# Forty dense blocks of a hybrid decoder step computed in pairs by seven half-size products

## The chip, the core and the metric

The kernel runs on one core of a Trainium2 chip. The metric is the device time of one execution in microseconds; the median of several runs is compared. One execution was also profiled: its records give the span from the first to the last instruction, the busy time of each engine and what each one waited for. The engines are named as in the profile: PE (TensorE, the matrix engine; PEld are its weight loads), DVE (VectorE), ACT (ScalarE), POOL (GpSimd) and SP (SyncE, which here issues all DMA transfers). Matmuls write to PSUM; PSUM is read by DVE and ACT, not by POOL.

## The reference, cut to what matters

One inference step of a decoder with two layers for 512 prompt tokens and 8 x 8 sample tokens, 576 in all, at width 2048. Layer A is gated linear attention, layer B a sliding-window attention.

```python
# layer A
proj = rmsnorm(h, g_norm) @ w_in                   # q, k, v, r (output gate), low-rank gate
o = rmsnorm(gla_chunked(q, k, v, logg, s0), g_onorm) * silu(r)
h = h + o @ w_out                                  # first output projection, 2048 x 2048
# layer B
k, v = split(rmsnorm(h, g_norm_kv) @ w_kv)
q, z = split(rmsnorm(h, g_norm_b) @ w_in)          # z: the last gates, 2048 x 2048
o = sink_attention(q, k, v) * silu(z)
h = h + o @ w_out                                  # last output projection, 2048 x 2048
y = rmsnorm(h, g_final)
```

All tensors are float32.

## The kernel before

The activations stand transposed in SBUF: 16 tiles `X[k]` of 128 features (the contraction) by 576 tokens, each as a high and a low part, since the product of two float32 matrices is made of three products of a shorter format: high x high, high x low, low x high. `HP` holds 16 tiles of the same shape in full float32, four to a tile. `halves` splits the 576 tokens into two sides of 288 (`HT`).

**Dense blocks.** `dense` (L184) makes one block, 128 outputs by 576 tokens. It loads the weights in two halves of 512 KB (`load_w`, L171), splits them by quarters of 128 x 512 (`split_w`, L167: a cast on ACT, then a subtraction on DVE), and issues 16 x 3 x 2 matmuls of 288 columns. The two sides of the tokens go to two PSUM banks, in turns. The quarters have `WB` = 4 buffers, so that ACT and DVE can be four quarters ahead of PE. At the end `evac` takes the block out of PSUM.

```python
def dense_mm(p, k, wh, wl, sides):
    x = X[k]
    for w, part in ((wh, 0), (wh, 1), (wl, 0)):
        for a in sides:
            mm(p[:, a, :HT], w, x[:, part, a * HT:(a + 1) * HT], ...)
```

**Stages.** 113 dense blocks follow one another, each of the following at a stretch: the projections of layer A (32 blocks), its output gates (`r_phase`, L665, 16 blocks), the first output projection (`out_a`, L691, 16 blocks with weights wOA), the shared K and V (4), the queries of layer B (`q_phase`, L975, 16), its gates (`z_phase`, L979, 16), and the last output projection (weights wOB, L1000 onward: 13 plain blocks, then 3 by halves of the tokens, 320 and 256 columns, so that norm and store of the first half run under the products of the second). Between stages `split_plain` or `split_gain` (L96 to L102) turn `HP` into the operands `X` of the next stage, one ACT and one DVE operation of 576 columns for each of 16 tiles.

**Side chains.** The recurrent part of layer A and the attention of layer B (`attention`, L952: 64 units of two heads and one block of queries, and 16 units for the samples, four in flight on the four PSUM banks of `bank`) are generators. `run` (L199) traces a dense stage and advances the side chains by a given number of steps for each step of it (0.95 for the attention); `drain` (L208) traces what is left of them. Tile orders the instructions of each engine when the program is built (`schedule_with_timeline_sim`, L1165): an instruction traced later can be put ahead of one that is not ready.

**Evictions.** A gate block is evicted in four steps: L984 (x 0.5 and the norm, from PSUM), a Tanh on ACT (L986), L987 and L988 on DVE (in layer A: L670 to L674). A block of the first output projection adds the residual (L700), which came by DMA, goes to DRAM as `dh1`, and its square is added to the sum for the next norm: L114 on ACT, L119 on POOL.

Of the kernel before, what the change touches and what calls it, by code (L numbers as in the profile page):

```python
# [17 lines left out]
D = 2048  # L18
NP = 512
NT = 576  # L20
# [17 lines left out]
def kernel(ctx: ExitStack, tc: tile.TileContext, A, O):  # L38
# [102 lines left out]
    def rstd_soon(srcs, n, b, lo, hi):  # L141
        """the same for the sum of srcs, left in the first bank of b; by columns, for few tokens"""
        toks = range(lo, hi, 128)
        col = sp.tile([128, 4], F32, tag="col", name=nm("col"))
# [9 lines left out]
        for i in range(m):  # L154
            dg = sp.tile([128, 128], F32, tag="dg", name=nm("dg"), bufs=2)
            vec.tensor_scalar(dg, ident, col[:, i:i + 1], None, ALU.mult)
            mm(p[:, i * 128:(i + 1) * 128], ones, dg, start=True, stop=True)
# [38 lines left out]

    bgs = []

    def run(fg):  # L199
        """trace fg, with the steps of the background chains between its own"""  # L200
# [17 lines left out]
    dqkb = [tc.dram_tile([6, 128, NT], F32, name=f"dqkb{h}") for h in range(NH)]  # L218
    dv = [tc.dram_tile([4, 128, NT], F32, name=f"dv{h}") for h in range(NH)]
    dh1 = tc.dram_tile([KT, 128, NT], F32, name="dh1")  # L220

    xT = A["xT"]
    rstdA = cp.tile([128, NT], F32, name="rstd", tag="rstd")

    with tc.tile_pool(name="gp", bufs=1) as gp:
        # ================= layer A ========================================
# [15 lines left out]
        rA2 = halves(rstdA)  # L242
# [21 lines left out]
        # low-rank gate: the columns [wh | wl] three times, so that the rows of its  # L264
        # output carry what the stacked operand of the next product needs
# [9 lines left out]
        # the first two blocks and the gate's product, together as x comes in  # L275
# [902 lines left out]
```

## Time and profile before

| what | value |
|---|---|
| median of 3 runs | 1792.68 us (1792.38 to 1793.38) |
| span of the profiled execution | 1791.2 us |
| PE busy, matmuls | 1767.2 us (99%), 13152 |
| DVE busy, instructions | 1117.0 us (62%), 2539 |
| ACT busy | 780.5 us (44%) |
| POOL busy | 110.1 us (6%) |
| granted PE clock, mean | 0.996 |
| HBM | 174.57 MB read, 43.65 MB written |

The span runs from the first to the last instruction; what a run's time has beyond it lies around the span. The times of three runs lie within 1.0 us. A busy share is a mean over all stages; the groups of rows below take single stages. A matmul's recorded duration holds the whole passage through the engine, and matmuls overlap, so that the distance between two starts is less than the duration.

### The profile page before, as it was taken

To read this page: it belongs to the slowest core of one execution; us is meant where nothing else is said; L and a number is where in the kernel's file an instruction comes from. 1 tells how busy PE (TensorE), PEld (TensorE's weight loads), DVE (VectorE), ACT (ScalarE), POOL (GpSimd) and SP (SyncE) were. 2 spreads that over 40 slices of the span, in tenths; PEclk is the share of its full clock that TensorE was granted. 3 is DMA by queue.
4 is the path that set the end of the run, shared out by engine and by line. 5 is a ranking of instruction groups with operands and counts; after the bars stand their busy time and mean duration, and the time that the engine had idled before them with its cause. 6 is when DMAs were issued, how large, how long until landed. Compare 5 with 4: busy or idle time off the path is not lost.

```text
span 1791.2 us, 33731 instructions
## 1 busy us (share of the span) xinstructions
PE 1767.2 (99%) x13152; PEld 1748.8 (98%) x13152; DVE 1117.0 (62%) x2539; ACT 780.5 (44%) x1632; POOL 110.1 (6%) x190
## 2 busy tenths in 40 slices
PE   8999999999999999999999999999999999999997
PEld 7999999999999999999999999999999999999996
DVE  8576776786776886544222566888888873442234
ACT  7533334334444344343222555667666652332231
POOL 3000001001001001000010100100000000001110
PEclk9999999999999999999999999999999999999998
DMA  8245643564564343223333444343332222223323
GB/s 301 89 160 176 195 156 117 176 197 136 161 194 158 119 154 135 96 77 124 128 131 127 134 134 110 88 126 101 105 99 88 85 94 82 83 98 108 104 106 106
DMA packets 118767, 231.02 MB, mean 129 GB/s; under 512 B 22064, under 2 KB 49584, under 8 KB 118576
## 3 DMA queue, kind: packets, MB, share of 16 engines
q1 hardware_dynamic: 118608, 228.88, 39.4%
q8 instruction: 103, 1.69, 0.4%
q14 instruction: 56, 0.46, 0.1%
HBM read 174.57 MB, written 43.65 MB: 122 GB/s over the span
## 4 chain that ended last, share of the span: by engine, by line
PE 94%; issue 2%; DMA 2%; DVE 1%; ACT 0%; POOL 0%; POOLq 0%; DVEq 0%; SPq 0%; ACTq 0%
PE pd L180 79%; PE pb L463 2%; PE pb L863 1%; PE pb L550 1%; DMA hp<-in_xT_dram 1%; PE pb L846 1%; PE pb L639 1%; PE pb L638 1%; PE pb L636 1%; PE pb L845 1%; PE pb L551 1%; PE pb L873 1%; PE pb L874 1%; PE pb L481 1%; PE pb L558 0%
## 5 line engine op out<-in xcount | busy, mean ns | idle before, releaser
L180 PE MATMUL pd<-x,wh 128*128 128x288 f32 x7232 | 1305.0, 298 | 9.8 <-ACT x L96 6.7
L180 PEld LDWEIGHTS pd<-x,wh 128*128 128x128 f32 x7232 | 1080.2, 189 | 17.4 <-ACT x L96 6.7
L180 PE MATMUL pd<-x,wl 128*128 128x288 f32 x3616 | 791.8, 298 | 0.7 <-DVE wl L169 0.6
L180 PEld LDWEIGHTS pd<-x,wl 128*128 128x128 f32 x3616 | 587.6, 189 | 4.1 <-DVE wl L169 1.4
L168 ACT CAST wh<-raw 128x512 fp32r<-128x512 f32 x452 | 279.4, 618 | 589.8 <-PE pd L180 577.5
L169 DVE TENSOR_TENSOR wl<-raw,wh 128x512 fp32r<-128x512 f32 x452 | 316.4, 701 | 337.7 <-ACT wh L168 336.1
L119 POOL TENSOR_TENSOR acc<-acc,st 128x576 f32<-128x576 f32 x46 | 70.3, 1528 | 323.2 <-ACT st L114 322.4
L855 ACT ACTIVATE s<-s,tiny 128x257 f32<-128x257 f32 (+1 forms) x128 | 60.9, 478 | 19.8 <-DVE tiny L853 19.6
L618 ACT CAST sh<-Si 128x512 fp32r<-128x512 f32 x64 | 39.7, 620 | 66.9 <-PE pb L638 43.9
L114 ACT ACTIVATE st<-hp 128x576 f32<-128x576 f32 (+2 forms) x66 | 43.3, 664 | 56.8 <-DVE hp L1045 28.6
L117 POOL COPY acc<-st 128x576 f32<-128x576 f32 x7 | 5.5, 779 | 907.6 <-ACT st L114 907.6
L640 DVE SCALAR_TENSOR_TENSOR Si<-Si,dl,pb 128x512 f32<-128x512 f32 x64 | 47.6, 744 | 12.2 <-PE pb L636 11.4
L619 DVE TENSOR_TENSOR sl<-Si,sh 128x512 fp32r<-128x512 f32 x64 | 44.4, 693 | 13.6 <-PE pb L639 5.5
L850 DVE SCALAR_TENSOR_TENSOR s<-distp,pb 128x256 f32<-128x256 f32 (+1 forms) x128 | 43.9, 383 | 11.2 <-PE pb L846 10.6
L867 ACT CAST pTh<-pb 128x256 fp32r<-128x256 f32 (+1 forms) x64 | 34.0, 532 | 29.7 <-PE pb L863 28.2
L868 DVE TENSOR_TENSOR pTl<-pb,pTh 128x256 fp32r<-128x256 f32 (+1 forms) x64 | 39.6, 620 | 8.4 <-ACT pTh L867 7.7
L878 ACT COPY hp<-pb 64x128 f32<-64x128 f32 x128 | 33.3, 260 | 25.5 <-PE pb L874 14.7
L438 ACT ACTIVATE E<-E 128x2304 f32<-128x2304 f32 (+1 forms) x20 | 37.5, 1875 | 15.3 <-DVE E L435 15.3
L97 DVE SCALAR_TENSOR_TENSOR x<-hp,c_vecs,x 128x576 fp32r<-128x576 f32 x48 | 42.1, 913 | 2.0 <-ACT x L96 2.0
L879 DVE TENSOR_TENSOR hp<-hp,pb 64x128 f32<-64x128 f32 x128 | 36.2, 283 | 9.2 <-ACT hp L878 6.6
L863 PE MATMUL pb<-c_ident,s 128*128 128x128 f32 x224 | 40.6, 273 | 0.0
L853 DVE TENSOR_REDUCE tiny<-s 128x2 f32<-128x258 f32 (+1 forms) x64 | 39.3, 616 | 1.7
(234 smaller groups left out, 1803.2 us busy)
## 6 DMA issues: line engine op xcount, KB each, us to landing
raw<-in_wA_dram SPq DMA_DIRECT2D x92, 512.0 KB
raw<-in_wB_dram SPq DMA_DIRECT2D x64, 512.0 KB
Si<-in_state_dram SPq DMA_DIRECT2D x64, 256.0 KB
out_gla_sample_dram<-Si SPq DMA_DIRECT2D x64, 256.0 KB
raw<-in_wOA_dram SPq DMA_DIRECT2D x32, 512.0 KB
raw<-in_wOB_dram SPq DMA_DIRECT2D x32, 512.0 KB
dqkb<-st SPq DMA_DIRECT2D x24, 288.0 KB
hp<-in_xT_dram SPq DMA_DIRECT2D x16, 288.0 KB
```

What stands on the lines that cost most here:

```text
L97: vec.scalar_tensor_tensor(t[:, 1, :], src, g, f32(t[:, 0, :]), ALU.mult, ALU.subtract)
L114: act(sq[:, lo:hi], src, AF.Square)
L119: self.eng.tensor_tensor(self.acc[:, lo:hi], self.acc[:, lo:hi], sq[:, lo:hi], ALU.add)
L168: nc.scalar.copy(wh, raw)
L169: vec.tensor_tensor(wl, raw, f32(wh), ALU.subtract)
L180: mm(p[:, a, :HT], w, x[:, part, a * HT:(a + 1) * HT], start=(k == 0 and w is wh and part == 0), stop=(k == KT - 1 and w is wl))
L618: nc.scalar.copy(sh, Si)
L619: vec.tensor_tensor(sl, Si, f32(sh), ALU.subtract)
L640: vec.scalar_tensor_tensor(Si, Si, dl[:, f * 16 + i:f * 16 + i + 1], p, ALU.mult, ALU.add)
L850: vec.scalar_tensor_tensor(s[:, e, off:256], distp[:, off:256], slope(2 * m + e), p[:, e * 256 + off:(e + 1) * 256], ALU.mult, ALU.subtract)
L855: act(s[:, e, off:257], s[:, e, off:257], AF.Exp, scale=-1.0, bias=tiny[:, e:e + 1], accum_out=tiny[:, 2 + e:3 + e])
L863: nc.tensor.transpose(out=p[:, (hf * 2 + e) * 128:(hf * 2 + e + 1) * 128], in_=s[:, e, off + hf * 128:off + (hf + 1) * 128], identity=ident)
```

## The change

Two neighbouring blocks (256 outputs), the 2048 features in two halves and the 576 tokens in two halves make a product of 2 x 2 by 2 x 2 parts. Before, it takes eight half-size products; now it takes seven, by Strassen's scheme in Winograd's form. Sums of weight halves (s1 to s4, eight additions of 128 x 512 per pair, on POOL, in place of the loaded weights) and sums of operand parts (t1 to t4, made once for each stage) come in addition, and the results are put together from the seven. Pairs are: all 16 blocks of wOA, gate blocks 4 to 15 of layer B, blocks 0 to 11 of wOB. Around them: the last six gate blocks of layer A move behind the release of that layer's memory, and the operand sums for wOA stand among them; the attention is drained after two gate blocks of layer B, two more plain ones follow with the operand sums of h read back from `dh1` (`sums_of_h`, `t1_of_h`), then come six gate pairs; before wOB `make_t` makes the operand sums of the gated attention; t1 takes the place of one operand part in `X`, so that the first half of the gated attention's second token half goes to DRAM (`dg2`) and is loaded again for the last four blocks, of which two (not three) go by halves. Sums of squares in the paired stages are added on DVE. The rest of the diff (removed comments, moved definitions) is left out.

```diff
+    PRODUCTS = {"A": ("w11", "x11", 0), "P4": ("w22", "t4", 1), "B": ("w12", "x21", 0),
+                "P5": ("s1", "t1", 2), "P6": ("s2", "t2", 3), "C": ("s4", "x22", 2),
+                "P7": ("s3", "t3", 1)}
+    ORDER = [(n, c) for n in ("A", "P4", "B", "P5", "P6", "C", "P7") for c in range(2)]
+    FIRST = [("A", 0), ("P4", 0), ("P5", 0), ("P6", 0), ("A", 1), ("P4", 1), ("B", 0), ("B", 1),
+             ("P5", 1), ("P6", 1), ("C", 0), ("C", 1), ("P7", 0), ("P7", 1)]
+    def dense_pair(wdram, blk, pool, evac, order=ORDER):
+        for name, b, hf in (("w11", 0, 0), ("w22", 1, 1), ("w12", 0, 1), ("w21", 1, 0)):
...
+        place = {"s1": "w22", "s2": "w11", "s3": "w21", "s4": "w12"}
...
+        def add(out, a, b, c):
+            nc.gpsimd.tensor_tensor(half(out, c), half(a, c), half(b, c), ALU.add)
+        def ready(c):
+            if ("w22", c) in split and ("s1", c) not in made:
+                add("s1", "w21", "w22", c)
+            if ("w11", c) in split and ("s1", c) in made and ("s2", c) not in made:
+                add("s3", "w11", "w21", c)
+                add("s2", "s1", "w11", c)
+            if ("w12", c) in split and ("s2", c) in split and ("s4", c) not in made:
+                add("s4", "s2", "w12", c)
+        for n, c in order:
...
+            split_w(half(w, c), wh, wl)
+            ready(c)
+            for kk in range(4):
+                for wt, part in ((wh, 0), (wh, 1), (wl, 0)):
+                    mm(p, wt[:, kk, :], xpart(x, k, part), ...)
...
+            if ends[n] == 2:
+                evac(n, p)
+    def make_t(g, lo, hi, tmp):
+        x11, x12, x21, x22 = lo[:, :, 0:HT], lo[:, :, HT:NT], hi[:, :, 0:HT], hi[:, :, HT:NT]
...
+        nc.gpsimd.tensor_tensor(t3, x22, x12, ALU.subtract)
+        vec.tensor_tensor(x12, x11, x12, ALU.subtract)
+        vec.tensor_tensor(t2, x12, x22, ALU.add)
+        nc.gpsimd.tensor_tensor(t4, t2, x21, ALU.subtract)
+        split("t4", t4)
+        split("t2", t2)
+        split("t3", t3)
+    def pair_out(j, r, ss, store):
+        def f(n, p):
...
+            elif n == "B":
+                vec.tensor_tensor(h[0][:, 0:HT], p, r[0][:, 0:HT], ALU.add)
...
+            elif n == "C":
+                vec.tensor_tensor(h[0][:, HT:NT], p, r[0][:, HT:NT], ALU.subtract)
+                ss.add(h[0])
+            elif n == "P7":
+                vec.tensor_tensor(h[1][:, 0:HT], r[1][:, 0:HT], p, ALU.subtract)
+                vec.tensor_tensor(h[1][:, HT:NT], h[1][:, 0:HT], tmp["a"][:, 1, :], ALU.add)
+                ss.add(h[1])
...
-        run(r_phase())
+        run(r_phase(range(RS)))
         drain()
+        for g, (a, b) in enumerate(((RS, RS), (RS, 12), (12, 14), (14, KT))):
+            run(r_phase(range(a, b)))
+            for _ in make_t(g, *two(g), tt):
+                pass
         for k in range(KT):
             split_plain(k, hpt(k))
-        ss = SumSq(nc.gpsimd)
+        ss = SumSq(vec)
+        run(out_pairs(A["wOA"], range(0, KT, 2), lambda j: xT[j * 128:(j + 1) * 128, :], ss, True))
...
+    def sums_of_h():
+        for g in range(4):
+            for k in (2 * g, 2 * g + 1):
...
+                    dma(x[i], dh1[kk])
+                    act(x[i], x[i], AF.Copy, scale=vecs[:, GB + kk:GB + kk + 1])
...
         bgs.append([attention(), 0.95, 0.0])
         run(q_phase())
-        run(z_phase())
+        run(z_phase(range(2)))
         drain()
-    NB = 3
+    NB, NS = 2, 12
+    with tc.tile_pool(name="zp", bufs=1) as zp:
+        bgs.append([sums_of_h(), 1.5, 0.0])
+        run(z_phase(range(2, 4)))
+        drain()
+        t1_of_h()
+        for j in range(4, KT, 2):
+            run(dense_pair(A["wB"], KT + j, zp, pair_z(j)))
+        for g in range(4):
+            for _ in make_t(g, *two(g), tt):
+                pass
         for k in range(KT):
             split_plain(k, hpt(k))
+        run(out_pairs(A["wOB"], range(0, NS, 2), lambda j: dh1[j], ss, False))
...
-        for j in range(KT - NB):
+        for j in range(NS, KT - NB):
             run(dense(A["wOB"], j, ev_o(j, resid(j))))
```

`RS` is 10. `pair_z` evicts a gate pair in the same way, with the norm, the Tanh and the product of L984 to L988 at the end.

## Rows read from the trace of the kernel before

**Rows 1.** The page, part 1: busy time, share of the span, instructions.
```profile
PE 1767.2 (99%) x13152; PEld 1748.8 (98%) x13152; DVE 1117.0 (62%) x2539; ACT 780.5 (44%) x1632; POOL 110.1 (6%) x190
```
**Rows 2.** The page, part 5, costliest groups: count, busy us, mean ns, idle before.
```profile
L180 PE MATMUL pd<-x,wh 128*128 128x288 f32 x7232 | 1305.0, 298 | 9.8 <-ACT x L96 6.7
...
L168 ACT CAST wh<-raw 128x512 fp32r<-128x512 f32 x452 | 279.4, 618 | 589.8 <-PE pd L180 577.5
```
**Rows 3.** Timeline of DVE in the first output projection: start us, us, instruction.
```profile
846.39 0.76 DVE L700 TENSOR_TENSOR hp<-pd,ld 128x576 f32<-128x576 f32 x1 [2.07 <-PE pd L180]
...
872.00 0.76 DVE L700 TENSOR_TENSOR hp<-pd,ld 128x576 f32<-128x576 f32 x1 [2.07 <-PE pd L180]
```
**Rows 4.** Timeline of PE, last blocks by halves, equal matmuls merged.
```profile
1739.70 4.56 PE L1041 MATMUL pd<-x,w 128*128 128x320 f32 x30
...
1763.20 13.30 PE L1041 MATMUL pd<-x,w 128*128 128x256 f32 x109
```
**Rows 5.** Timelines of POOL and DVE; then L169 as a line: ns min/median/max.
```profile
711.66 1.43 POOL L119 TENSOR_TENSOR acc<-acc,st 128x576 f32<-128x576 f32 x1 [1.49 <-ACT st L114]
...
712.05 1.58 DVE L169 TENSOR_TENSOR wl<-raw,wh 128x512 fp32r<-128x512 f32 x1 [0.41 <-ACT wh L168]
...
564.07 5.65 POOL L119 TENSOR_TENSOR acc<-acc,st 128x576 f32<-128x576 f32 x3
...
566.31 0.75 DVE L562 SCALAR_TENSOR_TENSOR S<-S,dl,pb 128x512 f32<-128x512 f32 x1
...
L169 DVE TENSOR_TENSOR wl<-raw,wh x452: 669/691/1923, 5.7 to 1727.7; 128x512 fp32r<-128x512 f32 x151
```
**Rows 6.** Line L453 (256 columns), and four queued operations of 576 columns.
```profile
L453 DVE TENSOR_TENSOR E<-E,kb x52: 414/419/423, 124.2 to 663.5; 128x256 f32<-128x256 f32 x52
...
800.72 2.76 DVE L102 TENSOR_TENSOR x<-hp,x 128x576 fp32r<-128x576 f32 x4
```
**Rows 7.** Windows: length, busy PE, PEld, DVE, ACT, POOL, clock, DMA share, GB/s.
```profile
100.00:270.00 170.00, 170.00 (x1235) 166.64 (x1235) 123.00 (x320) 61.30 (x108) 0.00 (x0) 1.00 0.54 174
820.00:1012.00 192.00, 192.00 (x1442) 192.00 (x1441) 59.40 (x85) 56.17 (x89) 20.56 (x15) 1.00 0.37 127
1402.00:1470.00 68.00, 68.00 (x534) 68.00 (x533) 55.34 (x147) 41.91 (x122) 3.27 (x15) 1.00 0.18 63
1720.00:1791.00 71.00, 58.26 (x436) 57.62 (x434) 31.33 (x67) 14.29 (x24) 3.58 (x3) 0.93 0.30 104
```
**Rows 8.** Groups by line in 1402 to 1470 us, dense work alone.
```profile
L180 PE MATMUL pd<-x,wh 128*128 128x288 f32 x263 | 48.8, 299 | 0.0
...
L180 PE MATMUL pd<-x,wl 128*128 128x288 f32 x131 | 29.6, 299 | 0.0
...
L169 DVE TENSOR_TENSOR wl<-raw,wh 128x512 fp32r<-128x512 f32 x17 | 11.6, 684 | 2.0 <-ACT wh L168 1.6 <-PE pb L863 0.3
...
L984 DVE SCALAR_TENSOR_TENSOR st<-pd,rstdB 128x576 f32<-128x576 f32 x5 | 3.8, 751 | 0.1
...
L987 DVE SCALAR_TENSOR_TENSOR st<-st,st 128x576 f32<-128x576 f32 x4 | 3.0, 753 | 0.0
L988 DVE TENSOR_TENSOR hp<-hp,st 128x576 f32<-128x576 f32 x4 | 3.0, 753 | 0.0
```
**Rows 9.** Last results of the attention (first and last start); gate evictions in 1338 to 1404.
```profile
L948 DVE TENSOR_TENSOR hp<-hp,t x32: 195/222/249, 1169.2 to 1468.7; 64x64 f32<-64x64 f32 x32
...
L984 DVE SCALAR_TENSOR_TENSOR st<-pd,rstdB 128x576 f32<-128x576 f32 x4 | 3.0, 748 | 0.3 <-PE pd L180 0.3
```
**Rows 10.** Timeline of DVE at the end: evictions of the last blocks by halves.
```profile
1758.96 0.49 DVE L1045 TENSOR_TENSOR hp<-pd,r 128x320 f32<-128x320 f32 x1 [5.46 <-PE pd L1041]
...
1775.66 0.42 DVE L1045 TENSOR_TENSOR hp<-pd,r 128x256 f32<-128x256 f32 x1
1776.53 0.42 DVE L1045 TENSOR_TENSOR hp<-pd,r 128x256 f32<-128x256 f32 x1 [0.46 <-PE pd L1041]
```

More of the change, by code (lines that the diff above doesn't have):

```diff
@@ L197, with out_pairs @@
+    def out_pairs(wdram, js, src, ss, store):
+        for j in js:
+            r = [tpool[0].tile([128, NT], F32, tag="ld", name=nm("ld"), bufs=2) for _ in range(2)]
+            for i in range(2):
+                dma(r[i], src(j + i))
+            yield from dense_pair(wdram, j, tpool[0], pair_out(j, r, ss, store), FIRST if j == 0 else ORDER)
     bgs = []
@@ L220, with r_phase, ev, f @@
     dh1 = tc.dram_tile([KT, 128, NT], F32, name="dh1")
+    dg2 = tc.dram_tile([8, 128, HT], F32, name="dg2")
+    dt1 = tc.dram_tile([8, 128, HT], F32, name="dt1")
     xT = A["xT"]
     rstdA = cp.tile([128, NT], F32, name="rstd", tag="rstd")
+    rA2 = halves(rstdA)
+    norm_done = [False] * NH
+    def r_phase(js):
+        def ev(j):
+            def f(p):
+                assert norm_done[j // 4]
+                rs = st()
+                vec.scalar_tensor_tensor(halves(rs), p, 0.5, rA2, ALU.mult, ALU.mult)
+                th = st()
+                act(th, rs, AF.Tanh)
+                vec.scalar_tensor_tensor(rs, th, 1.0, rs, ALU.add, ALU.mult)
+                vec.scalar_tensor_tensor(hpt(j), hpt(j), vecs[:, GO + j:GO + j + 1], rs, ALU.mult, ALU.mult)
+            return f
+        for j in js:
+            yield from dense(A["wA"], 32 + j, ev(j))
+    RS = 10
     with tc.tile_pool(name="gp", bufs=1) as gp:
@@ L241 @@
         bmask = const("bmask", [128, 4])
-        rA2 = halves(rstdA)
         def evac_to(dst, scale):
@@ L663, in gla_samples @@
                 norm_done[h] = True
-        def r_phase():
-            def ev(j):
-                def f(p):
-                    assert norm_done[j // 4]
-                    rs = st()
-                    vec.scalar_tensor_tensor(halves(rs), p, 0.5, rA2, ALU.mult, ALU.mult)
-                    th = st()
-                    act(th, rs, AF.Tanh)
-                    vec.scalar_tensor_tensor(rs, th, 1.0, rs, ALU.add, ALU.mult)
-                    vec.scalar_tensor_tensor(hpt(j), hpt(j), vecs[:, GO + j:GO + j + 1], rs, ALU.mult, ALU.mult)
-                return f
-            for j in range(KT):
-                yield from dense(A["wA"], 32 + j, ev(j))
         bgs.append([gates(), 0.5, 0.0])
@@ L718, with gate, z_phase, ev @@
     dk = tc.dram_tile([4, 2, 64, NT], F32, name="dk")
+    units_done = [0]
+    def gate(j, rs):
+        th = st()
+        act(th, rs, AF.Tanh)
+        vec.scalar_tensor_tensor(rs, th, 1.0, rs, ALU.add, ALU.mult)
+        vec.tensor_tensor(hpt(j), hpt(j), rs, ALU.mult)
+        if j < 8:
+            dma(dg2[j], hpt(j)[:, HT:NT])
+    def z_phase(js):
+        def ev(j):
+            def f(p):
+                assert units_done[0] >= min(20 * (j // 4) + 23, 82)
+                rs = st()
+                vec.scalar_tensor_tensor(halves(rs), p, 0.5, rB2, ALU.mult, ALU.mult)
+                gate(j, rs)
+            return f
+        for j in js:
+            yield from dense(A["wB"], KT + j, ev(j))
@@ L720, with t1_of_h @@
+    def t1_of_h():
+        for g in range(4):
+            t = tt()
+            dma(t, dt1[2 * g:2 * g + 2].rearrange("a p t -> p a t"))
+            for i in range(2):
+                o = X[2 * g + i]
+                nc.scalar.copy(o[:, 0, HT:NT], t[:, i, :])
+                vec.tensor_tensor(o[:, 1, HT:NT], t[:, i, :], f32(o[:, 0, HT:NT]), ALU.subtract)
     with tc.tile_pool(name="ap", bufs=1) as ap:
@@ L1054 @@
             else:
-                r = rstd_soon([ss.acc, sq], D, (1, 2, 3), lo, hi)
+                r = rstd_soon([ss.acc, sq], D, (1, 2, 3), lo, hi, tp)
             for j in range(KT):
```

185 lines of the change are left out of this document (149 added, 36 removed).

## Prediction

> **What bounds the kernel now.** I read the busy times first: TensorE (PE) is busy 99% of a span of 1791.2 us, VectorE (DVE) 62% [rows 1]. The median run is 1792.7 us, 1.5 us above that span, and I add the 1.5 to whatever the span becomes. Next I read the costliest groups: dense matmuls of 288 columns on line 180 are most of PE's list, and each group of four weight tiles costs one cast of 618 ns on ScalarE (ACT) and one subtraction of about 0.69 us on DVE [rows 2, 5]. Busy time of a pipelined engine is no price, so the price of a matmul comes from a timeline: from one eviction to the second after it is 25.61 us for 192 matmuls, 133.4 ns each [rows 3]. PE is full in every dense stage [rows 7], so each matmul saved there is worth 133.4 ns, as long as PE stays full. The question is whether it does.
>
> **What is removed.** A pair of blocks takes 2 x 96 = 192 matmuls now, and 7 products x 8 contraction tiles x 3 = 168 then: 24 fewer. 20 pairs (8 in the first output projection, 6 in the gates, 6 in the last projection) save 480 x 133.4 ns = **64.0 us**. The shape stays 128x288. What differs is that consecutive matmuls go to one PSUM bank where they alternated between two. The last blocks do that already: 30 of 320 columns in 4.56 us are (4.56 - 0.31) / 29 = 147 ns apart, and 109 of 256 columns in 13.30 us about 121 ns [rows 4]. Between them 288 columns fall at 134 ns, so the bank costs nothing.
>
> **Inside a pair: +4 us in all (0 to 52).** PE needs 168 x 0.1334 = 22.4 us. ACT has 14 casts at 0.62 and some five small operations, 11.3 us. DVE operations of 576 columns start 0.67 us apart when queued, (2.76 - 0.75) / 3, against 0.75 us alone; so I take 0.605 us for 512 columns and, between 0.42 us for 256 and 0.69 for 512 columns, 0.45 alone and 0.37 queued for 288 [rows 5, 6]. An output pair then costs DVE 14 x 0.605 + 7 x 0.37 + 2 x 0.67 = 12.4 us, a gate pair 8.5 + 6 x 0.37 + 5 x 0.67 = 14.0. GpSimd (POOL) gets eight weight sums and one or three small ones; by its 1.43 us for 576 columns that is 1.27 and 0.71 us, 12.3 us for an output pair and 10.9 for a gate pair [rows 5]. Each fits in 22.4 us alone. But the two do not run side by side. While POOL added from 711.66 to 713.09, a DVE subtraction with both inputs in SBUF that began at 712.05 took 1.58 us where the median is 0.69: it ended 0.54 us after the addition. One that took an input from PSUM in the midst of three POOL additions kept its 0.75 [rows 5]. With 0.55, and by columns 0.31 and 0.61 us, for DVE operations of 512, 288 and 576 columns, the shared input is taken 12.3 + 9.85 = 22.15 us of 22.4 in an output pair and 10.9 + 11.4 = 22.3 in a gate pair. It fits, barely. Weights are split up to four groups ahead of PE (6.4 us), which absorbs single waits, so I charge 0.2 us a pair. If every duration counted in full the sums would be 24.8 and 25.2 us, the upper bound: 14 x 2.4 + 6 x 2.8 = 50 us.
>
> The Trainium skill's page "SBUF — State Buffer", section "Who interferes with whom", says that a DVE instruction with two SBUF inputs and a GpSimd instruction that reads SBUF exclude one another for a whole instruction, and that one SBUF input does not contend. The trace agrees: 1.58 us against 0.69, and 0.75 with a PSUM input [rows 5]. By that rule read to the letter the pairs last 24.8 and 25.2 us, and the change gains almost nothing in them.
>
> Transfers stay hidden: a pair moves 2.1 MB of weights and at most 1.2 MB else in 22.4 us, 147 GB/s, where one stage held 174 with PE full [rows 7]. The fourth weight half has one buffer, which comes free with the last product; SP then holds everything queued behind that load, but its data are first added for the fifth product of the next pair, about 10 us of PE later.
>
> **Into the first output pairs: +2 us (0 to 5).** The 16 operand splits stand in both kernels and start under the last gate block. New are the sums of operands, three quarters of them under gate blocks that leave DVE idle. The last quarter hangs on the last gate block: four eviction steps, a POOL sum of 1.43, a DVE difference, a cast and a subtraction of about 0.7 each make some 7 us, and PE has 6.4 us of other quarter products before it needs them.
>
> **Out of the attention: +36 us (27 to 77), the largest term.** Attention runs as a side chain between dense blocks. Today its last results come at 1468.7 us, and four gate blocks have been evicted by 1404 and four more by 1470 (five evictions lie in 1402 to 1470, the first of them the fourth block's) [rows 8, 9]: dense gate blocks run far ahead and fill PE while DVE works through the attention. The change leaves four plain gate blocks. All gate pairs need operand sums that are made after the attention frees its memory, and its four PSUM banks. So from about 1402 us the cover is gone. In 1402 to 1470 DVE was busy 55.3 us, of which 11.6 + 3.8 + 3.0 + 3.0 = 21.4 are dense work; 33.9 are attention. PE did 394 dense matmuls, 52.6 us, so attention is 15.4 us of PE [rows 7, 8]. Without dense work this tail lasts between 33.9 us (DVE without a pause) and 68 (as now), and leaves PE idle 18.5 to 52.6 us. I take DVE at 95%, 35.7 us, since the queue of dense matmuls that its inputs stand behind is gone too: 20.3 idle. Then come the sums: 8 x 7 DVE operations of 288 columns, 20.7 us, eight more for the part that goes through DRAM, 3.0, eight weight splits, 4.8, and some 2 us for the first load: 30.5 us. PE has nine quarter products of 1.6 us for that time, 14.4; so 16 idle (9 if loads and splits hide, 24 if only the first four quarters can run).
>
> **Into the last output pairs: +8 us (5 to 16).** Here no gate block covers the sums. From the start of the last gate pair to the end of the first output pair PE has 44.8 us; DVE has 28 weight splits (16.9), the evictions of this pair and the end of the one before (9.5), 8 differences and 12 splits for the sums (13.3), 16 operand splits (10.7) and 1.5 more: 51.9 us. The 7 us over are PE's wait, and POOL's locks add to it.
>
> **Smaller edits.** Into the K/V projection: the operands come free early, +1 (0 to 3). End: two blocks by halves in place of three. After the first half's products end at 1758.9, its norm and scaling keep DVE until 1775.7, and the second half's products last until 1776.5 [rows 10]. With two blocks these last only 96 x 0.121 = 11.6 us and DVE still 17, while the first half ends 12.8 - 48 x 0.147 = 5.8 us later: +5 (0 to 6). Reloading eight half operands hides behind the first plain block's other half. Sums of squares move from POOL to DVE and are counted above.
>
> **Sum.** -64.0 + 4 + 2 + 36 + 8 + 1 + 5 = -8: 1792.7 - 8 = **1784.7 us**. On its own bounds this case runs from 1761 to 1800.
>
> **Rivals.** *The cover holds.* Attention ends by the fourth gate block, because only its order fixed at build time, not its engines, held it back; the sums hide under the plain blocks. For: DVE idles 12.7 us in that stretch. Against: with PE empty of dense work, 33.9 us of DVE remain. Then 36 falls out: 1748.7. Chance 0.25. *The tail keeps its pace* (slower): attention's last units go on at today's 68 us, for each waits on ACT, DVE and PE in turn. For: DVE is only 81% busy there [rows 7]. Against: those waits are partly behind dense matmuls. Idle 52.6 in place of 20.3: 1817. It decides once the tail lasts over 44 us. Chance 0.22. *The shared input binds* (slower): pairs at 24.8 to 25.2 us, 50 for 4: 1831. For: 99% occupancy. Against: overlap of 0.14 us per operation. Chance 0.11. That the matmuls are not fewer is excluded by the code, and their pitch by [rows 4].
>
> **Numbers.** A difference under 0.2% (3.6 us) cannot be told from none. Forecast 0.42: of it 0.28 below 1789.1, 0.11 within, 0.03 above. Faster is 0.28 + 0.25 = 0.53; same, with 0.03 for a tail between the cases, 0.14; slower 0.03 + 0.19 + 0.11 = 0.33. The range, 1749 to 1820, leaves out the shared-input case and little else. PE's clock in the idle stretches adds to the high side: it was granted 0.93 in the last stretch, where PE was busy 58.3 of 71 us, against 1.00 in full ones [rows 7].
>
> **What would show it.** About 12,670 matmuls; output pairs 22.4 to 22.8 us apart; POOL busy some 200 us more (237 for the pairs, less 30 sums of squares), with DVE subtractions above 1 us; two stretches with PE far from full, one after the fourth gate block of 30 to 40 us, one of 8 us before the last projection; a granted clock below 1 in them. Pairs at 25 us, or no gap behind the attention, would prove the forecast wrong.

## The result, and the profile after

The changed kernel takes 1905.9 us (median of 4 runs, 1904.1 to 1907.1) against 1792.5: a ratio of 1.063 with a 95% interval of 1.061 to 1.064. I had forecast 1784.7 and a range of 1749 to 1820, so both the sign and the range were wrong. The first part of the profile after answers to [rows 1]. Its columns are the busy time, its share of the span (1902.3 us) and the instructions:

```profile
PE 1755.5 (92%) x12672; PEld 1711.9 (90%) x12672; DVE 1443.3 (76%) x2898; ACT 907.8 (48%) x1891; POOL 402.9 (21%) x385
```

The 480 matmuls are gone, as the code says. What PE gained it lost in waiting. The stretches by stage, as in [rows 7] (length, busy PE, PEld, DVE, ACT, POOL, granted clock, DMA share, GB/s), of the kernel after:

```profile
844.00:989.00 145.00, 137.62 (x1018) 134.99 (x1017) 112.91 (x140) 63.40 (x115) 91.45 (x66) 1.00 0.42 137
989.00:1018.00 29.00, 24.65 (x170) 23.94 (x169) 24.95 (x31) 19.77 (x34) 15.99 (x11) 0.94 0.30 100
1408.00:1448.00 40.00, 26.41 (x134) 21.23 (x133) 34.64 (x106) 27.17 (x89) 2.89 (x16) 0.74 0.01 5
1448.00:1515.00 67.00, 34.47 (x175) 29.38 (x175) 46.69 (x97) 36.26 (x79) 13.88 (x10) 0.65 0.48 154
1515.00:1619.00 104.00, 92.53 (x677) 89.71 (x676) 92.61 (x102) 42.13 (x76) 57.17 (x36) 1.00 0.26 87
1619.00:1646.00 27.00, 22.92 (x170) 22.21 (x169) 26.91 (x28) 14.15 (x26) 18.11 (x12) 1.00 0.21 69
1646.00:1705.00 59.00, 34.32 (x167) 29.90 (x167) 47.99 (x62) 24.20 (x41) 29.32 (x16) 0.65 0.12 42
1705.00:1824.00 119.00, 113.83 (x843) 111.67 (x842) 101.25 (x116) 52.69 (x95) 77.68 (x55) 1.00 0.33 109
1824.00:1902.00 78.00, 56.83 (x402) 55.77 (x401) 36.24 (x76) 17.66 (x32) 0.72 (x1) 0.86 0.37 125
```

Three stretches stand out, where PE is busy 34 of 67, 34 of 59 and 26 of 40 us: the first gate pair (1448 to 1515), the first pair of the last projection (1646 to 1705), and the attention's end before both (1408 to 1448). In the steady gate pairs DVE, not PE, has hardly a pause (92.6 of 104, then 26.9 of 27 us).

The pairs themselves are measured from a pair's first matmul on line 274 to the next pair's (168 matmuls of 133 ns would be 22.4 us). I add up what each part of the kernel costs beyond that, beside the terms of my sum:

| part | forecast (range) | after | excess over PE's time, us |
|---|---|---|---|
| 480 matmuls | -64 | 12672 matmuls | -64 |
| first output pair | +2 (0 to 5) | 36.6 | +14.2 |
| 16 steady pairs | +4 (0 to 52; for all 20 pairs) | 22.95 to 24.4 (output), 25.9 to 27.1 (gates), 23.1 to 24.2 (last) | +35 |
| last output pair, into K/V | +1 (0 to 3) | 29.4 | +7 |
| from K/V to the gate pairs | +20.3 of the +36 (27 to 77) | 430.1, before 405.0 | +25 |
| first gate pair | +16 of the +36 | 67.1 | +44.7 |
| first pair of the last projection | +8 (5 to 16) | 59.3 | +36.9 |
| end | +5 (0 to 6) | 78.1, before 66.5 | +12 |
| sum | -8 | | +111 |

The 405.0 of before are the 558.6 us from the last matmul of the first output projection to the last of the gates, less 12 gate blocks of 12.8 us, in whose place the gate pairs stand. The spans of the two profiled executions differ by 111.1 us, the medians by 113: the account by place closes. What made each excess is the question of the experiments.

**In the pairs** the shared input shows. The lines of POOL's weight sums, of the splits and of PE's waits in 868 to 989 us, five output pairs (count, busy us and mean ns, idle before and why):

```profile
L169 DVE TENSOR_TENSOR wl<-raw,wh 128x512 fp32r<-128x512 f32 x70 | 70.3, 1034 | 27.2 <-ACT wh L168 26.8
...
L244 POOL TENSOR_TENSOR raw<-raw,raw 128x512 f32<-128x512 f32 x40 | 61.0, 1547 | 39.7 <-DMA raw<-in_wOA_dram 23.6 <-DVE acc L119 8.1 <-DVE wl L169 7.2
...
L274 PE MATMUL pb<-t,wh 128*128 128x288 f32 x240 | 49.1, 297 | 3.3 <-ACT wh L168 3.3
...
L168 ACT CAST wh<-raw 128x512 fp32r<-128x512 f32 x71 | 43.4, 618 | 64.2 <-POOL raw L244 38.2 <-PE pb L274 26.0
...
L274 PE MATMUL pb<-t,wl 128*128 128x288 f32 x120 | 35.9, 299 | 3.6 <-DVE wl L169 3.6
```

The split, 0.69 us in [rows 5], takes 1.03 on average, and ACT's casts now wait 38.2 us for POOL's sums. PE waits 6.9 us in these five pairs, about half of it for low splits and half for casts that stand behind POOL's sums. How the two engines meet is seen in a gate pair. First POOL's timeline of 1541 to 1556 us, equal instructions merged:

```profile
1541.47 13.43 POOL L244 TENSOR_TENSOR raw<-raw,raw 128x512 f32<-128x512 f32 x8 [7.64 <-DVE wl L169]
```

Then DVE's timeline of the same stretch (start, us, instruction; no bracket means no idle time before it):

```profile
1543.63 1.54 DVE L928 TENSOR_TENSOR st<-st,tt 128x288 f32<-128x288 f32 x1
1545.10 1.77 DVE L169 TENSOR_TENSOR wl<-raw,wh 128x512 fp32r<-128x512 f32 x1
1546.79 1.84 DVE L929 SCALAR_TENSOR_TENSOR st<-st,rstdB 128x576 f32<-128x576 f32 x1
1548.56 1.78 DVE L169 TENSOR_TENSOR wl<-raw,wh 128x512 fp32r<-128x512 f32 x1
1550.26 1.84 DVE L884 SCALAR_TENSOR_TENSOR st<-st,st 128x576 f32<-128x576 f32 x1
1552.02 1.75 DVE L169 TENSOR_TENSOR wl<-raw,wh 128x512 fp32r<-128x512 f32 x1
1553.69 1.83 DVE L885 TENSOR_TENSOR hp<-hp,st 128x576 f32<-128x576 f32 x1
```

Eight sums come in one run of 13.4 us, 1.68 us each, and in that run DVE gets one operation through per sum, one every 1.7 us where it starts one every 0.6 to 0.67 alone. PE comes through the first 8 us of the run without a wait and then waits for the low splits (from its timeline of the same stretch; the bracket is the wait before the matmul):

```profile
1550.39 0.40 PE L274 MATMUL pb<-x,wl 128*128 128x288 f32 x1 [0.80 <-DVE wl L169]
...
1553.82 0.41 PE L274 MATMUL pb<-x,wl 128*128 128x288 f32 x1 [1.57 <-DVE wl L169]
```

Over 1515 to 1619 us, four gate pairs, this is PE's only wait:

```profile
L274 PE MATMUL pb<-x,wl 128*128 128x288 f32 x128 | 39.0, 304 | 11.5 <-DVE wl L169 11.5
```

**Into the first gate pair** PE waits for the sums of the normalised input. All its waits of 1448 to 1515 us (total us, times, longest):

```profile
PE pb L274 <- ACT t L950: 26.7, 7, 10.1
PE pb L274 <- DVE t L951: 3.7, 3, 2.5
PE pb L274 <- ACT x L969: 1.9, 1, 1.9
```

### The profile page after: what moved, and what is told of

It reads as the page before. It is cut to its first block, busy times and chain, and to the rows that moved or that the text cites. A ratio compares the mean times of both kernels' runs of the same rounds, so it can differ in the third digit from the quotient of the medians.

```text
span 1902.3 us, 34005 instructions
## 1 busy us (share of the span) xinstructions
PE 1755.5 (92%) x12672; PEld 1711.9 (90%) x12672; DVE 1443.3 (76%) x2898; ACT 907.8 (48%) x1891; POOL 402.9 (21%) x385
## 4 chain that ended last, share of the span: by engine, by line
PE 68%; DVE 10%; issue 8%; POOL 6%; DMA 4%; ACT 2%; POOLq 0%; DVEq 0%; SPq 0%; ACTq 0%
PE pd L180 47%; PE pb L274 8%; POOL raw L244 6%; DVE wl L169 3%; PE pb L648 2%; DMA raw<-in_wOA_dram 2%; PE pb L1115 1%; PE pb L734 1%; DVE x L102 1%; DMA raw<-in_wOB_dram 1%; PE pb L823 1%; PE pb L820 1%; PE pb L822 1%; PE pb L735 1%; PE pb L1098 1%
## 5 line engine op out<-in xcount | busy, mean ns | idle before, releaser
L180 PE MATMUL pd<-x,wh 128*128 128x288 f32 x4736 | 871.0, 299 | 14.0 <-ACT x L96 6.9
L180 PEld LDWEIGHTS pd<-x,wh 128*128 128x128 f32 x4736 | 714.4, 190 | 22.1 <-ACT x L96 6.9
L169 DVE TENSOR_TENSOR wl<-raw,wh 128x512 fp32r<-128x512 f32 x576 | 490.3, 864 | 166.2 <-ACT wh L168 158.4
L180 PE MATMUL pd<-x,wl 128*128 128x288 f32 x2368 | 523.5, 298 | 0.9 <-DVE wl L169 0.9
L180 PEld LDWEIGHTS pd<-x,wl 128*128 128x128 f32 x2368 | 387.2, 190 | 3.9 <-DVE wl L169 1.2
L244 POOL TENSOR_TENSOR raw<-raw,raw 128x512 f32<-128x512 f32 x160 | 259.4, 1641 | 178.9 <-DVE wl L169 94.9
L274 PE MATMUL pb<-x,wh 128*128 128x288 f32 x1280 | 270.9, 304 | 27.2 <-ACT x L101 11.3
L274 PE MATMUL pb<-t,wh 128*128 128x288 f32 x960 | 205.4, 305 | 46.1 <-ACT t L950 26.7
L274 PEld LDWEIGHTS pb<-x,wh 128*128 128x128 f32 x1280 | 213.6, 195 | 31.9 <-DVE x L102 12.9
L274 PE MATMUL pb<-x,wl 128*128 128x288 f32 x640 | 194.6, 305 | 18.5 <-DVE wl L169 18.5
L274 PEld LDWEIGHTS pb<-t,wh 128*128 128x128 f32 x960 | 159.0, 193 | 54.3 <-ACT t L950 29.4
L824 DVE SCALAR_TENSOR_TENSOR Si<-Si,dl,pb 128x512 f32<-128x512 f32 x64 | 47.5, 743 | 11.5 <-PE pb L820 11.2
```

The source lines that it names most:

```text
L169: vec.tensor_tensor(wl, raw, f32(wh), ALU.subtract)
L180: mm(p[:, a, :HT], w, x[:, part, a * HT:(a + 1) * HT], start=(k == 0 and w is wh and part == 0), stop=(k == KT - 1 and w is wl))
L244: nc.gpsimd.tensor_tensor(half(out, c), half(a, c), half(b, c), ALU.add)
L274: mm(p, wt[:, kk, :], xpart(x, k, part), start=(opens and first and kk == 0 and wt is wh and part == 0), stop=(ends[n] == 2 and kk == 3 an ...
L824: vec.scalar_tensor_tensor(Si, Si, dl[:, f * 16 + i:f * 16 + i + 1], p, ALU.mult, ALU.add)
```

## The experiments

Experiments 1 to 4, 8 and 9 were timed once, the others four times, and times of one kernel lie up to 8 us apart: a few us between two totals show nothing. The lengths of pairs come from one profiled execution each. Where nothing was changed they repeat within 1 us: the first output pair takes 36.6 and 36.5 us and the first of the last projection 59.3 and 59.4 in the kernel after and in experiment 4; the first gate pair 67.1 and 67.9 in the kernel after and in experiment 3.

**1. The weight sums on VectorE.**

```diff
-            nc.gpsimd.tensor_tensor(half(out, c), half(a, c), half(b, c), ALU.add)
+            vec.tensor_tensor(half(out, c), half(a, c), half(b, c), ALU.add)
```

> The 160 weight sums go from POOL to VectorE; nothing else changes. Theory (POOL and VectorE hold each other up at SBUF): the sums take about 0.70 us each on VectorE, the lo split of line 169 goes back from a mean of 864 ns to about 700, VectorE is then busy 17 to 19 us of a pair, so the steady pairs go to 22.4 to 22.9 us (now 24.2 in both output stages and 25.9 in the gates), and the two transitions give something too, since POOL's queue holds operand sums alone: 1845 to 1870 us in all. Rival (the chain split, sum, split is simply too long, or VectorE becomes the bound): pairs stay at 24 us or more and the time is 1895 to 1925 us.

Measured: 1860.0 us. Steady pairs of all three kinds take 22.3 us. The stretches of six output pairs, five gate pairs and the first pair of the last projection (columns as above):

```profile
848.00:982.00 134.00, 134.00 (x1013) 134.00 (x1012) 110.45 (x187) 65.71 (x114) 52.01 (x18) 1.00 0.46 149
...
1500.00:1611.00 111.00, 111.00 (x838) 111.00 (x837) 101.03 (x166) 56.69 (x101) 7.56 (x7) 1.00 0.31 101
1611.00:1669.00 58.00, 36.05 (x169) 31.52 (x168) 45.45 (x70) 24.87 (x42) 23.80 (x8) 0.65 0.12 38
```

PE is full in the first two, although DVE now makes the sums as well. In the gate stretch DVE is busy 101 of 111 us, and that is enough. The first pairs hardly moved, though: 33.5 (from 36.6), 66.1 (from 67.1) and 58.2 us (from 59.3). So the weight sums explain the 35 us of the steady pairs and some 5 of the 7 into K/V, and not the ways into a stage.

**2. The weight sums left out.** The line above goes without a substitute.

> The 160 weight sums are left out altogether (the products take the raw halves of the block), everything else stays. Theory: nothing then holds the lo splits, all steady pairs take 22.4 us, the 168 matmuls' own time, and the first gate pair and the attention's end stay as long as they are (67 us for the pair, 1448 us for its start less what the output pairs gain): 1840 to 1865 us. Rival (the pairs are held by something other than the sums, as the evictions or the loads): pairs stay above 24 us and the time falls by under 15 us, to over 1890.

Measured: 1845.7 us, steady pairs 22.3 us, first pairs 31.4, 63.9 and 51.1. The steady pairs are no shorter than with the sums on VectorE, so there they are free. The other side of it: even with no weight sums at all the three ways in (operand sums unchanged) cost 9, 42 and 29 us more than PE's time.

**3. The operand sums on VectorE**, the weight sums still on POOL.

```diff
-        nc.gpsimd.tensor_tensor(t3, x22, x12, ALU.subtract)
+        vec.tensor_tensor(t3, x22, x12, ALU.subtract)
...
-        nc.gpsimd.tensor_tensor(t4, t2, x21, ALU.subtract)
+        vec.tensor_tensor(t4, t2, x21, ALU.subtract)
```

> The operands t3 and t4 of both output projections (8 operations of 2 x 128 x 288) go from POOL to VectorE; the weight sums stay on POOL. Theory (at the way into the last output pairs the operand sums stand in POOL's queue behind the weight sums of the blocks to come): the first pair of the last output projection falls from 59.3 us to 45 to 52, the very first pair of the kernel from 36.6 to 31 to 35, and steady pairs stay at 24.2 and 25.9: 1888 to 1900 us. Rival (VectorE is what the way in waits for): the first pairs stay within 2 us, or grow, and the time is 1902 to 1912 us.

Measured: 1899.5 us, inside the theory's range; first pairs 32.8 and 52.8 us, the first inside what the theory gave, the second 0.8 us above it. POOL's part in the ways in is real but small: 4 and 7 us.

**4. More plain gate blocks under the attention.**

```diff
-        run(z_phase(range(2)))
+        run(z_phase(range(6)))
...
-        run(z_phase(range(2, 4)))
+        run(z_phase(range(6, 8)))
...
-        for j in range(4, KT, 2):
+        for j in range(8, KT, 2):
```

> Eight plain gate blocks in place of four: six under the attention in place of two, then two under the sums of the normalised input, and four pairs in place of six. Theory (the attention's tail and those sums lost their cover): the attention's tail is filled again, its 26.5 us go to 3 or less, the first gate pair takes 27 to 32 us in place of 67, and the two pairs that become plain cost next to nothing, since a gate pair takes 25.9 us and two plain blocks 25.6: 1838 to 1850 us. Rival (the attention runs as fast as it can and the sums wait for their loads, whatever lies beside them): the gate stages keep their length and the time stays within 15 us of 1906.

Measured: 1872.1 us, between the two. The attention's tail is covered again: PE is busy without a break to 1473 us. But the first gate pair still takes 60.7 us, against 27 to 32 expected. The rows show why. In this kernel the last result of the attention (line 1200), the last plain gate eviction (line 894) and the scalings that begin the sums (line 941) start at (min/median/max ns, then first and last start):

```profile
L1200 DVE TENSOR_TENSOR hp<-hp,t x32: 196/222/251, 1173.6 to 1473.7; 64x64 f32<-64x64 f32 x32
...
L894 DVE SCALAR_TENSOR_TENSOR st<-pd,rstdB x8: 742/750/758, 1357.1 to 1474.0; 128x576 f32<-128x576 f32 x8
...
L941 ACT ACTIVATE xg<-xg,c_vecs x16: 758/773/776, 1477.0 to 1512.3; 128x576 f32<-128x576 f32 x16
```

The instruction order fixed at build time spread the tail over all eight plain blocks, and the sums, whose tiles lie in the attention's memory, began when it ended, with no plain block left. In the kernel after the attention had ended at 1455.4, without cover, against 1468.7 before [rows 9]: the tail runs faster alone, though not for nothing.

**5. All sums on VectorE** (edits 1 and 3 together).

> Both earlier edits together: the weight sums and the operands t3, t4 all on VectorE. Theory: with the weight sums on VectorE alone the way into the last output pairs still took 58.2 us, and there POOL's t4 took 5.7 and 6.2 us where one alone takes 1.4, since VectorE worked without a break; so the operand sums on VectorE too bring the first pair there to 38 to 48 us and the very first pair from 33.5 to 28 to 32, steady pairs at 22.3: 1838 to 1851 us. Rival (VectorE's own queue is what the ways in wait for, whoever makes t3 and t4): first pairs within 3 us of 58.2 and 33.5, 1854 to 1864 us.

Measured: 1850.2 us, ratio to before 1.033 (1.031 to 1.034); first pairs 31.8 and 53.1 us. The time and the first of the two are in the theory's range; 53.1 lies between the ranges of theory and rival, so POOL's stretched t4 was a part (5 us) of the way into the last projection, not the bulk.

**6. All 16 gates plain**, on top of edit 5; the sums of the normalised input fall away.

```diff
-        bgs.append([sums_of_h(), 1.5, 0.0])
-        run(z_phase(range(2, 4)))
-        drain()
-        t1_of_h()
-        for j in range(4, KT, 2):
-            run(dense_pair(A["wB"], KT + j, zp, pair_z(j)))
+        run(z_phase(range(4, KT)))
```

> As the version with all sums on VectorE, but all 16 gate blocks plain, so that the sums of the normalised input go too and both output projections alone go by pairs. Theory: the gates get back before's 153.6 us and the attention's tail its cover (22 us), against 24 us (gate stage) plus 22 us now, so some 46 us less than the version with gate pairs: 1790 to 1808 us, no longer slower than before by more than 1%. Rival (the attention's tail stands open because of something else, such as the pools' memory): the tail keeps its 22 us and the time is 1815 us or more.

Measured: 1778.7 us, ratio 0.992 (0.990 to 0.993): faster than before, and 11 us below the range I gave. What I had not counted is that the first pair of the last projection falls as well, from 53.1 to 32.2 us.

**7. Two plain blocks first in each projection**, on top of edit 6. X is split from the untouched operands, the two blocks run, t1 is fetched from DRAM into x12's place, then the pairs follow. The operand sums of the last projection are also written between the last gate blocks; the sums themselves moved little by it: the first sums of the four groups start at 1486, 1511, 1536 and 1564 us in experiment 6 and at 1482, 1507, 1532 and 1561 us here.

```diff
+        for k in range(KT):
+            split_plain(k, hpt(k))
+        for j in range(2):
...
+            yield from dense(wdram, j, ev(j, r))
+        t1_of_h()
+        yield from out_pairs(wdram, js, src, ss, store)
```

> As with plain gates, and two of each projection's blocks go plain and first, so that t2, t3, t4 and the weight sums are made under them; t1 waits in DRAM and replaces x12 behind the last plain block. Theory (what the ways in cost is operand work that lay open): each projection loses one pair (3.3 us) and its way in falls to before's 8 to 10 us, the first pairs take 22.3 to 25 us: 1760 to 1782 us, faster than before by 0.6 to 1.8%. Rival (the operand work fills VectorE so that the plain blocks before and at the way in take longer by as much): 1788 us or more.

Measured: 1763.9 us, ratio 0.984 (0.983 to 0.986), inside the theory's range. All pairs but the last before K/V take 22.3 us, the first ones too. The last gates, the plain blocks and the pairs of the last projection, and the end:

```profile
1360.00:1553.00 193.00, 193.00 (x1498) 193.00 (x1497) 135.95 (x288) 99.31 (x237) 6.23 (x24) 1.00 0.30 95
1553.00:1579.00 26.00, 26.00 (x202) 26.00 (x202) 22.14 (x38) 12.49 (x25) 0.00 (x0) 1.00 0.40 133
1579.00:1690.00 111.00, 111.00 (x839) 111.00 (x839) 90.98 (x152) 54.28 (x95) 37.93 (x15) 1.00 0.38 116
1690.00:1768.00 78.00, 56.51 (x400) 55.41 (x398) 35.90 (x75) 17.82 (x32) 0.72 (x1) 0.88 0.37 123
```

PE is full from 1360 us to the end of the last pair. The ways in cost nothing any more.

**8. Two gate pairs behind twelve plain gates**, on top of edit 5.

```diff
-        run(z_phase(range(2)))
+        run(z_phase(range(8)))
...
-        run(z_phase(range(2, 4)))
+        run(z_phase(range(8, 12)))
...
-        for j in range(4, KT, 2):
+        for j in range(12, KT, 2):
```

> As the version with all sums on VectorE, but twelve plain gate blocks (eight under the attention, four under the sums of the normalised input) and two gate pairs. Theory (in the version with eight plain blocks the sums began at 1477 us, right behind the attention's end at 1473.7, where the plain blocks had run out: their tiles lie in the memory that the attention frees): with four plain blocks left behind the attention the first gate pair takes 23 to 28 us in place of 66, the tail is covered, and four pairs less cost 13 us: 1790 to 1812 us. Rival (a first pair waits for its operands wherever the sums are, by their chain of loads, scaling and splits): the first gate pair stays over 45 us and the time over 1820.

Measured: 1794.6 us, the first gate pair 24.7 us. So the sums cost PE 2 us once plain blocks run behind the attention's end, and experiment 4 had failed for want of such blocks. The first pair of the last projection still takes 52.7 us here, behind only two gate pairs, against 32.2 behind plain gates. The stretch of that wait, columns as above:

```profile
1549.00:1587.00 38.00, 19.77 (x71) 15.45 (x69) 37.88 (x61) 18.43 (x31) 0.00 (x0) 0.59 0.00 0
```

DVE's costliest lines in it (count, busy us and mean ns, idle before):

```profile
L290 DVE TENSOR_TENSOR t<-tt,t 128x576 fp32r<-128x576 f32 x12 | 8.6, 745 | 0.0
L102 DVE TENSOR_TENSOR x<-hp,x 128x576 fp32r<-128x576 f32 x12 | 8.5, 744 | 0.0
L169 DVE TENSOR_TENSOR wl<-raw,wh 128x512 fp32r<-128x512 f32 x8 | 5.4, 679 | 0.1
L244 DVE TENSOR_TENSOR raw<-raw,raw 128x512 f32<-128x512 f32 x8 | 5.3, 676 | 0.0
```

DVE is busy 37.9 of 38 us. All twelve splits of t2, t3 and t4 (line 290) stand here: behind plain gates only the last three do (three on line 290 from 1557 to 1590 us with plain gates). A gate pair reads the old t2, t3 and t4 up to its last product, the new ones go to the same tiles, and X is read as long. That the tiles are the reason is argued from the code; the full queue is what the rows show.

**9. Idle additions on POOL.** Edit 5, and behind each weight sum on VectorE:

```diff
+            for q in (0, 2):
+                y = half(out, c)[:, q:q + 2, 0:120]
+                nc.gpsimd.tensor_tensor(idle, y, y, ALU.add)
```

> The version with all sums on VectorE (steady pairs 22.3 us, 1850 us), and behind each of its 160 weight sums POOL adds the new half to itself, in two pieces of 128 x 240, into a tile that nothing reads: POOL works beside VectorE about as long as when it made the sums, but nothing waits for it. Theory (while POOL reads SBUF, VectorE's operations on two SBUF inputs stand, and the other way about): the lo splits of line 169 go back from 0.69 to a mean of 0.80 to 0.90 us, steady pairs to 23.5 to 25 us (output) and 24 to 26 us (gates), 1875 to 1900 us in all. Rival (it was the longer way through POOL, 1.3 to 1.6 us for a sum in place of 0.68, in the chain split, sum, split): pairs stay at 22.3 to 22.5 us, 1847 to 1855 us.

Measured: 1934.8 us, some 85 above edit 5 and outside both ranges, on the theory's side. Steady pairs: 24.7 to 27.4 us (output), 25.2 to 26.0 (gates), 25.1 to 26.9 (last). The lines of POOL's additions, DVE's splits and DVE's weight sums in 1542 to 1670 us:

```profile
L248 POOL TENSOR_TENSOR idle<-raw 128x240 f32<-128x240 f32 x80 | 73.5, 919 | 52.3 <-DVE raw L245 35.4 <-issue 11.6 <-POOL idle L248 0.7
...
L169 DVE TENSOR_TENSOR wl<-raw,wh 128x512 fp32r<-128x512 f32 x68 | 62.4, 938 | 0.0
...
L245 DVE TENSOR_TENSOR raw<-raw,raw 128x512 f32<-128x512 f32 x40 | 31.8, 810 | 0.3 <-DMA raw<-in_wB_dram 0.3
```

Nothing in the program waits for these additions but the release of a weight buffer, and yet the split goes back to 0.94 us and the pairs to 25 and more. Late weights are not what held the splits: DVE has no pause before them in these rows. So POOL's reading beside DVE is enough to lengthen the pairs, without POOL in the chain of sums. That POOL's longer way in that chain cost nothing besides is not shown: in the output pairs above, 3.3 of PE's 6.9 us of waits stood behind casts of POOL's sums. It came out worse than the theory's numbers because DVE now carries the weight sums too, and they are held up as well (0.81 us against 0.68).

**10. x12 restored beside the last pair**, on top of edit 7.

```diff
+        for g in range(4):
+            t = zp.tile([128, 2, 2, HT], F32R, tag=f"t4{g}", name=nm("g2"))
+            for i in range(2):
+                o, y = X[2 * g + i], f32(t[:, i, 0, :])
+                dma(y, dg2[2 * g + i])
...
-        for k in range(8):
-            t = tp.tile([128, HT], F32, tag="g2", name=nm("g2"), bufs=4)
-            dma(t, dg2[k])
```

> As with a plain block first in each projection, and x12, which the last four blocks read again, comes back from DRAM into the tiles that t4 leaves, beside the last pair, instead of behind it. Theory (the end is 12 us longer than before's because PE waits 3.7 us and more for the first x12 and then goes on at the low clock): the end after the last pair falls from 78 us to 66 to 70: 1751 to 1758 us. Rival (the end is held by the weights and residuals of the last blocks, whose tiles also open late): 1761 to 1766 us.

Measured: 1762.5 us (1757.7 to 1765.4), ratio 0.983 (0.981 to 0.985). The time is in the rival's range and doesn't tell it from edit 7 (1763.9). The stage in the profile does, 72.1 us in place of 78.0, between the theory's 66 to 70 and no gain:

```profile
1684.00:1756.00 72.00, 54.30 (x399) 53.68 (x397) 32.30 (x67) 14.49 (x24) 0.72 (x1) 0.88 0.34 117
```

PE's wait for the restored operands (3.7 us in experiment 7) is gone. Of its waits that are left, one was much shorter before; first this kernel's, then that of the kernel before (total us, times, longest):

```profile
PE pb L148 <- ACT st L1318: 5.3, 1, 5.3
```

```profile
PE pb L148 <- DVE acc L119: 0.8, 1, 0.8
```

Half of the end's 12 us was the restore. The other 6 stay, and most of them is this wait for the squares of the very last results, which fits the forecast's +5 for two blocks by halves; no run goes back to three blocks by halves to test it. In the profiled executions the stretch ahead of the first pair, nearly the same in edits 1, 2, 5, 6 and 8, ended anywhere between 805 and 815 us, and a gain of 6 is hard to see beside that.

**11. Two gate pairs again**, in the kernel of edit 10.

> As the version before, but with twelve plain gates and two gate pairs, and the two plain blocks of the last projection between these pairs and its own. Theory (behind gate pairs VectorE has some 47 us of operand work in one piece, since X and t2, t3, t4 are read to the last pair's end; two plain blocks cover what isn't needed at once): the way in costs 8 to 16 us in place of 30, the two gate pairs give 6.6, so 1753 to 1766 us, about as much as without gate pairs. Rival (VectorE's queue is in order, and the splits of the plain blocks stand behind all of that work): the way in keeps 25 us or more, 1770 us or more.

Measured: 1770.2 us (1768.2 to 1772.7), ratio 0.987 (0.986 to 0.989): above the theory's range and at the very start of the rival's. The stages say otherwise. From the start of the second gate pair to that of the second pair of the projection is 81.6 us, with two pairs and two plain blocks of PE's time in it, 70.1: the way in costs 11.5, as the theory had it (8 to 16) and less than half of the rival's 25, and the way into the gate pairs 4.3. Against 6.6 us saved that is a loss of 9, and the medians differ by 7.6. My total started too low, from the 1755 expected of edit 10.

## Why the prediction was wrong

**What held.** 480 matmuls fewer at 133.4 ns: the steady pairs run at 22.3 us once nothing holds them. The places were right too: two stretches with PE far from full, behind the attention and ahead of the last projection, low granted clocks there, splits above 1 us. Every cost in the sum was too small, and four of them by more than the bounds I gave.

**Inside a pair, +4: measured 35.** The step that failed is "weights are split up to four groups ahead of PE (6.4 us), which absorbs single waits". I had found the lock and added up its occupancy (22.15 and 22.3 of 22.4 us) as if it were spread over the pair. The sums come in runs, 13.4 us in the row above, in which DVE's rate falls to a third; four groups last 6.4, and PE's waits begin 8 us into the run. Experiment 1 takes the 35 us away; experiment 9, where no product needs what POOL adds, puts some 56 back. How much of the 35 was POOL's longer way in the chain stays open. The pairs of 24.8 and 25.2 us that I kept as an upper bound and gave 0.11 came close in the output pairs (24.2) and were passed in the gates (25.9). The Trainium skill's page "SBUF — State Buffer", section "Who interferes with whom", holds that whoever issues first keeps the shared ports for its whole instruction and the other blocks fully. Read to the letter, as the forecast quoted it, it gave those 24.8 and 25.2; the trace agrees better with that than with my +0.2 a pair. One measurement goes beyond that rule: a waiting POOL addition was passed by 47 operations of VectorE (last section).

**Out of the attention, +36: measured 70.** The tail was near (25 for 20.3). The step that failed is the price of the sums: 44.7 us for 16. I had PE do nine quarter products meanwhile and bounded the wait by DVE's 30.5 us. In fact the sums ran from 1458.8 to 1496 us and their t1 to 1501: eight times two loads, two scalings, four differences and three splits, with DVE busy 46.7 of 67 us: no engine was full, so occupancy was no bound. PE's order is fixed at build time, and it waited for whichever split came next, up to 10.1 us. The clock, which the forecast left without a price, is a small part: 29 of the pair's matmuls start 0.24 us after the one before in place of 0.133 (granted clock 0.65 in the stretch), some 3 us. No run separates loads, buffers and splits in that chain; experiment 8 shows only that it hides, all but 2 us, under plain blocks.

**Into the last output pairs, +8 (5 to 16): measured 37.** I counted 51.9 us of DVE against 44.8 of PE, from the start of the last gate pair. That DVE could begin then is what failed: of its work the operand splits, 28 at 0.67 us or 19 in all, start only near the pair's end (the first at 1640.8 us, where the pair ends at 1646.1); that they wait for X, t2, t3 and t4 to come free is argued from the code. So PE waits for that queue 30 us even with nothing left on POOL (experiment 8), after plain gates 10 (experiment 6), behind two plain blocks not at all (experiment 7).

**First output pair, +2: measured 14; into K/V, +1: 7; end, +5: 12.** The first is the same fault on a smaller scale: the operand work of the last gate block lay open for 9 us with all sums off POOL (31.8 us in experiment 5), and two plain blocks cover it. K/V's was mostly the weight sums on POOL: 24.7 us with them on VectorE, 2.4 open. In the end, "reloading eight half operands hides behind the first plain block's other half" failed: that block begins with the operands being restored, and PE waited for them (6 us of the 12, experiment 10).

**The rivals.** "The cover holds" needed plain blocks behind the attention. "The tail keeps its pace" was wrong (attention ended 13 us earlier than before without cover). "The shared input binds" was right in kind and was given 0.11: 35 us measured of its 50. By itself it would have made at most 1831, and the ways in made the rest.

**Left open.** Whether gate pairs could pay with a second set of tiles for t2, t3 and t4 (twelve of 4.6 KB a partition) wasn't tried.

The step from 1905.9 to 1762.5, added up: weight sums off POOL -45.9, operand sums off POOL -9.8, gates plain -71.5, plain blocks first -14.8, restore -1.4 (6 in its stage; the two medians alone don't tell it from nothing). The last kernel keeps 12 of the 20 pairs and gains 1.7% on before.

## What to carry to other kernels

A saving on the engine that bounds a kernel is worth its time only in the steady state; price each way into a stage by asking when the tiles of the new operands come free and which queue then holds all their work, since an engine whose order is fixed gets no cover from work that stands behind the wait. Keep a stretch of the old, operand-free work (plain blocks here) at each such place: two of them cost 3.3 us a stage and took away 9 and 10. And where two engines exclude one another, don't add their occupancies: look at how the work arrives, in runs or spread, and if one of the two can hold all of it, give it all of it.

## What the runs showed that I had not expected

**A lone addition on POOL can wait out VectorE's whole queue.** In the way into the last projection of experiment 1, POOL's t4 of 576 columns, an addition of 1.43 us in [rows 5], took 5.7 and 6.2 us. Its timeline there:

```profile
1623.86 5.66 POOL L298 TENSOR_TENSOR tt<-tt,hp 128x576 f32<-128x576 f32 x1 [5.01 <-DVE tt L296]
1629.48 1.40 POOL L293 TENSOR_TENSOR tt<-hp,hp 128x576 f32<-128x576 f32 x1
1636.82 6.17 POOL L298 TENSOR_TENSOR tt<-tt,hp 128x576 f32<-128x576 f32 x1 [5.94 <-ACT x L101]
```

And DVE's, from the same stretch:

```profile
1636.58 0.68 DVE L169 TENSOR_TENSOR wl<-raw,wh 128x512 fp32r<-128x512 f32 x1
1637.18 1.41 DVE L102 TENSOR_TENSOR x<-hp,x 128x576 fp32r<-128x576 f32 x2
1638.52 0.68 DVE L244 TENSOR_TENSOR raw<-raw,raw 128x512 f32<-128x512 f32 x1
...
1640.99 0.74 DVE L290 TENSOR_TENSOR t<-tt,t 128x576 fp32r<-128x576 f32 x1
1643.73 1.24 DVE L290 TENSOR_TENSOR t<-tt,t 128x576 fp32r<-128x576 f32 x1 [2.00 <-ACT t L289]
```

DVE's operations keep their 0.68 to 0.74 us, back to back, and POOL's addition ends at 1642.99, 1.26 us after DVE's queue first paused (1641.73). In experiment 9 an idle addition that began at 1680.10 needed 30.6 us, while 47 DVE operations started. The long waits end alike: in the kernel after, experiment 1 and experiment 9, each of the 20 additions on POOL that took over 3 us ended 0.45 to 1.34 us after DVE first paused or first started an operation with an input from PSUM.

Yet in a run of POOL's additions (1541 us, above) the two take turns, one for one, and in experiment 9 an addition that began at 825.71 beside a DVE without a pause was through in 0.97 us. So a burst on POOL slows DVE to a third, and a full queue on DVE can stop POOL altogether. What decides whether the turn is given no run shows.
